# Two-layer attention trunk: weight loads woven between units, the row of 1/rms by a matmul with ones, five plain pairs, and earlier scores in layer 1

## The chip, the cores and the metric

One core of a Trainium2 chip runs the whole program in one launch. Its engines each have an instruction queue of their own: TensorE (PE, with PEld for its weight loads), VectorE (DVE), ScalarE (ACT), GpSimd (POOL) and SyncE (SP, which issues most transfers). They wait for one another through semaphores only. The metric is device time in microseconds; 0.2% of it is 2.8 us.

## The reference

The input is x, 512 tokens by 1024 channels. Two layers, each attention and then a dense FFN, both behind an RMSNorm and added to x; a final RMSNorm:

```
for i in range(2):
    h = rmsnorm(x, norm_mix[i])
    x = x + (window_gqa_sink(h, ...) if i == 0 else dilated_mixture_attention(h, ...))
    h = rmsnorm(x, norm_ffn[i])
    x = x + (silu(h @ w_gate[i]) * (h @ w_up[i])) @ w_down[i]      # 1024 -> 2816 -> 1024
return rmsnorm(x, norm_final)
```

Layer 0 is windowed attention with 16 query and 4 key heads. Layer 1 has three groups of heads (windows 128, 512 and 2048; strides 1, 4 and 16), each with its own q, k and v of 16 heads, merged by softmax weights.

## The kernel before, in words

All is held transposed, 128 channels by 512 tokens a tile. Each fp32 operand is split into a high and a low part (fp32r): ACT copies the high part, DVE subtracts to get the low one. `mm3` (L121) multiplies high by high, high by low and low by high, in pieces of 256 columns, so a `unit` (L204) of 128 output channels is 8 k-steps of 6 matmuls, 48 in all. `load` (L104) fetches a unit's weights (SP) and splits them: `wh` on ACT (L97), `wl` on DVE (L98). The weight pool has three buffers of each.

The order on PE is written out by hand everywhere: generators yield after each k-step (a slot), and `spread`, `weave` and `chain` put steps of attention between slots. The other engines are put in order by a scheduler that takes, among the instructions that are ready by its own clock, the one that comes first in the program. Only in the first part of each FFN are DVE and ACT kept in program order too (`ORDERED`, L855 and L931).

RMSNorm is put off: matmuls run on x times its gain, and results are scaled by 1/rms per token. `squares` (L263) adds up x*x in `ssum` (POOL). `norm_sums` (L296) sums over the channels by matmuls with one column of ones, which gives a number per token on partitions, and computes 1/rms there on tiles of 4 columns. `norm_rows` (L305) turns these into a row repeated on all partitions (`rb`) by four PE transposes and an ACT copy.

**Layer 0** runs k, q and v of the first heads, then attention in 16 blocks, each woven with a stretch of `fill` (L489): the other q and k units and the first output units. **Layer 1** runs q and k of group 0, then the four values units of group 0 (64 slots), then the attention steps `attention_a(0)` (scores, merge, turns, weighted sum) among further units (`fillers`, L1297). The numbers in `waits` (L1246) are the slots between the steps.

**The FFN** (`swiglu`, L585) has 22 pairs of a gate and an up unit. The first `plain` (6) pairs are plain units (`conventional`, L863). The others are made by a Strassen scheme of 7 products of half a unit's length, 12 matmuls each (`product`, L710), which needs sums and differences of the input, made on DVE in 19 steps (`input_steps`, L633: 8 `normed`, then splits `parts` and subtractions `less`) within the plain pairs, by `make`. Per pair f, in program order: load of up(f); `combined(f-1)` (two DVE multiplies); `make` or `kept(f-1)` (a split); load of gate(f+1); `gated(f)` (a DVE multiply and Silu); `make`. In the last plain pair, the weight sums of the first Strassen pair take the place of the loads: `h12 l12 f5`, `h64 l64 f7`, `h57 l57`, `h3 l3` (h on ACT, l and f on DVE). The third product of a Strassen pair uses `h57` and `l57`. Gate(1) and up(1) here mean the units of pair 1.

## Time and profile before

| | us |
|---|---|
| median of 3 runs | 1396.22 (1395.93 to 1396.76) |
| the profiled execution | 1396.07 |
| its span, first to last instruction | 1394.3 |
| PE busy in it | 1382.5 (99%) |
| DVE busy | 855.4 (61%) |
| ACT busy | 681.9 (49%) |
| POOL busy | 225.2 (16%) |

Busy PE is not PE at its peak: matmuls are pipelined, and one that is shown as 276 ns starts some 113 ns after the one before it. So read the starts of matmuls for its pace, and look at the gaps for its waits.

### The profile page before, as it was taken

The page shows a single profiled execution, that of the slowest core. Times are in us where ns is not written, and L with a number is a line of the kernel's source. Part 1 is how long each engine was busy: PE and PEld are TensorE (multiplying, and loading weights), DVE is VectorE, ACT ScalarE, POOL GpSimd, SP SyncE. Part 2 cuts the span into 40 slices and gives each one's busy share as a digit, 9 for nine tenths or more (in the row PEclk, how much of TensorE's full clock was granted, in tenths as well). Part 3 has the DMA queues.
Part 4 walks back from the last instruction along what each step waited for, and adds up shares of the span by engine and source line. Part 5 has one row for each costly group of instructions (what it writes and reads, how often), then busy time and mean ns, then how long its engine had stood idle before and what let it go on. Part 6 is the DMA issues. An engine that isn't in the chain of part 4 may idle for free.

```text
span 1394.3 us, 29677 instructions
## 1 busy us (share of the span) xinstructions
PE 1382.5 (99%) x12414; PEld 1367.2 (98%) x12414; DVE 855.4 (61%) x1593; ACT 681.9 (49%) x1250; POOL 225.2 (16%) x318
## 2 busy tenths in 40 slices
PE   9999999999999999999999999999999999999998
PEld 8988999999999999999999999999999999999998
DVE  6876558853687456345656556646466884388633
ACT  6866534632556356435545436436354462265522
POOL 1233320100110111011112111211132010021022
PEclk9999999999999999999999999999999999999999
DMA  6110263752683232322122222222136383387122
GB/s 203 61 62 16 77 184 104 188 138 99 183 201 92 89 110 94 107 77 92 62 93 80 73 92 76 78 83 71 62 110 179 112 212 105 106 210 194 65 95 73
DMA packets 61063, 153.63 MB, mean 110 GB/s; under 512 B 8320, under 2 KB 14336, under 8 KB 60928
## 3 DMA queue, kind: packets, MB, share of 16 engines
q1 hardware_dynamic: 49888, 134.28, 29.1%
q0 software_dynamic: 10752, 16.92, 7.6%
q8 instruction: 97, 1.59, 0.5%
q10 hardware_dynamic: 288, 0.52, 0.1%
q14 instruction: 38, 0.31, 0.1%
HBM read 149.52 MB, written 2.17 MB: 109 GB/s over the span
## 4 chain that ended last, share of the span: by engine, by line
PE 93%; DVE 3%; ACT 2%; issue 1%; SPq 0%; DMA 0%; POOL 0%; DVEq 0%; ACTq 0%
PE mm L126 38%; PE mm L714 12%; PE sc L126 11%; PE psv L126 9%; PE sc L714 9%; PE tp L126 5%; PE ov L431 1%; PE sc L1140 1%; PE ovb L1195 1%; PE sc L1081 1%; PE tp L1103 1%; ACT pr L407 1%; PE ov L1122 1%; DVE pr L400 1%; PE sc L148 1%; DVE wl L98 1%
## 5 line engine op out<-in xcount | busy, mean ns | idle before, releaser
L98 DVE TENSOR_TENSOR wl<-wraw,wh 128x1024 fp32r<-128x1024 f32 (+5 forms) x196 | 211.6, 1084 | 193.3 <-ACT wh L97 190.4
L97 ACT ACTIVATE wh<-wraw 128x1024 fp32r<-128x1024 f32 (+3 forms) x195 | 181.6, 937 | 240.4 <-PE mm L126 132.2
L126 PE MATMUL mm<-xh,wh 128*128 128x256 f32 x1320 | 267.2, 282 | 0.6 <-ACT xh L259 0.6
L126 PE MATMUL mm<-xl,wh 128*128 128x256 f32 x1320 | 260.9, 278 | 0.1
L126 PE MATMUL mm<-xh,wl 128*128 128x256 f32 x1320 | 260.5, 277 | 0.0
L126 PEld LDWEIGHTS mm<-xh,wh 128*128 128x128 f32 x1320 | 201.6, 189 | 2.5 <-ACT xh L259 0.9
L126 PEld LDWEIGHTS mm<-xl,wh 128*128 128x128 f32 x1320 | 201.0, 189 | 0.7 <-DVE xl L260 0.6
L126 PEld LDWEIGHTS mm<-xh,wl 128*128 128x128 f32 x1320 | 200.8, 189 | 0.0
L671 POOL DMA_DIRECT2D w<-wunits x64 | 56.1, 907 | 417.8 <-DVE wl L694 165.9
L126 PE MATMUL psv<-wh,xh 128*128 128x256 f32 x288 | 80.7, 280 | 0.0
L126 PE MATMUL psv<-wl,xh 128*128 128x256 f32 x288 | 79.9, 277 | 0.2 <-DVE wl L98 0.2
L126 PE MATMUL psv<-wh,xl 128*128 128x256 f32 x288 | 79.8, 277 | 0.0
L273 POOL TENSOR_TENSOR ssum<-ssum,tmp 128x512 f32<-128x512 f32 x26 | 45.8, 1762 | 180.3 <-ACT tmp L270 118.8
L714 PE MATMUL mm<-bh,wh 128*128 128x256 f32 x256 | 70.7, 276 | 0.0
L714 PE MATMUL mm<-bl,wh 128*128 128x256 f32 x256 | 70.7, 276 | 0.0
L714 PE MATMUL mm<-bh,wl 128*128 128x256 f32 x256 | 70.7, 276 | 0.0
L714 PE MATMUL sc<-bh,wh 128*128 128x256 f32 x256 | 70.7, 276 | 0.0
L714 PE MATMUL sc<-bl,wh 128*128 128x256 f32 x256 | 70.7, 276 | 0.0
L714 PE MATMUL sc<-bh,wl 128*128 128x256 f32 x256 | 70.7, 276 | 0.0
L714 PE MATMUL mm<-bh,h 128*128 128x256 f32 x256 | 70.7, 276 | 0.0
L714 PE MATMUL mm<-bl,h 128*128 128x256 f32 x256 | 70.7, 276 | 0.0
L714 PE MATMUL mm<-bh,l 128*128 128x256 f32 x256 | 70.7, 276 | 0.0
(242 smaller groups left out, 3716.0 us busy)
## 6 DMA issues: line engine op xcount, KB each, us to landing
wraw<-wunits SPq DMA_DIRECT2D x159, 512.0 KB, 3.2
w<-wunits SPq DMA_DIRECT2D x96, 256.0 KB, 4.9
w<-wunits POOLq DMA_DIRECT2D x64, 256.0 KB, 5.7
wraw<-wv SPq DMA_DIRECT2D x25, 512.0 KB, 3.3
wraw<-wunits SPq DMA_DIRECT2D x28, 192.0 KB, 2.4
x<-xT SPq DMA_DIRECT2D x8, 256.0 KB, 5.2
wraw<-wunits SPq DMA_DIRECT2D x3, 256.0 KB, 5.8
wraw<-wunits SPq DMA_DIRECT2D x2, 384.0 KB, 2.9
```

The lines of the kernel that those rows point to most:

```text
L97: nc.scalar.activation(out_h, src, AF.Copy)
L98: nc.vector.tensor_tensor(out_l, src, out_h.bitcast(F32), op=OP.subtract)
L126: nc.tensor.matmul(out[:, cols], a, b[:, cols], start=first and k == 0 and c == 0, stop=last and k == 2, skip_group_check=True)
L148: nc.tensor.matmul(outs[a], qp[a][:, qc], k[a][:, kc], start=first and k is kp, stop=k is low, skip_group_check=True)
L273: eng.tensor_tensor(norm["sum"], norm["sum"], sq, op=OP.add)
L400: nc.vector.tensor_tensor_reduce(out=pr[:, e, :w], in0=ps[hf], in1=tab0[:, off:off + w], scale=SLOPES[heads[e]], scalar=-3e38, op0=OP.add, ...
L407: nc.scalar.activation(pr[:, e, :w + 1], pr[:, e, :w + 1], AF.Exp, bias=m[:, 1, e:e + 1], accum_out=m[:, 2, e:e + 1])
L431: nc.tensor.matmul(ov[64 * hf:64 * hf + 64, 256 * n:256 * n + 256], v0[:, k0 // 128 + kb, vs], st["pt", kb][:, 256 * hf:256 * hf + 256], s ...
L671: nc.gpsimd.dma_start(sums[:, 512 * k:512 * k + 512], v[:, 0:512], accum_op=OP.add)
L714: nc.tensor.matmul(out, a[:, j], b[:, j], start=first and j == 0 and i == 0, stop=j == 3 and i == 2, skip_group_check=True)
L1081: nc.tensor.matmul(out, qk["qs", p][a][:, 128 * t:128 * t + 128], kp[k], start=t == ts[0] and k == 0, stop=k == 1, skip_group_check=True)
L1103: nc.tensor.transpose(tp[:, (nb * a + kb) * 128:(nb * a + kb) * 128 + 128], st["pr", p, ts][:, a, o + 128 * kb:o + 128 * kb + 128], ident)
```

## The change

1. In layer 0, the units behind the first values are built with `ahead=True` and chained by a new generator, `staggered`: it starts each next unit, and so its load, when the unit before is half done, and not when it ends. PE's order stays.
2. In both FFNs, `norm_direct` replaces `norm_sums` and `norm_rows`. It splits `ssum` into two parts (ACT, DVE), and four matmuls of 256 columns with a 128x128 tile of ones give the sum over channels on all partitions at once. 1/rms is then computed on 128x512 tiles (five DVE operations and one on ACT), where it was computed on 128x4 tiles. On PE it stands behind the first k-step of up(0). `gated(0)` and the first `normed` come before the rest of up(0).
3. `plain` is 5 instead of 6, in both FFNs.
4. In layer 1, the two scores and the merge of `attention_a(0)` come among the values units 2 to 4, and the slots between its later steps are reset. The number of slots up to its end stays at 49.

```
--- before.py
+++ after.py
@@ -189,6 +189,19 @@
                     gens.append(makers[k + 2]())
                     next(gens[-1][1])
                 yield
+
+    def staggered(n, gen, makers):
+
+
+        for make in (*makers, None):
+            for c in range(n):
+                if c == n // 2 and make:
+                    after = make()
+                    next(after[1])
+                next(gen)
+                yield
+            if make:
+                n, gen = after
 
     def last_outputs(out_part, at, fill=()):
 
@@ -311,6 +324,31 @@
         rb = norm["rb"] = spool.tile([128, S], F32, name="rb", bufs=1)
         cols = slice(128 * blocks[0], 128 * blocks[-1] + 128)
         nc.scalar.activation(rb[:, cols], pr[:, cols], AF.Copy)
+        for done in norm["wait"] or ():
+            done()
+        norm["wait"] = None
+
+    def norm_direct(pool, between):
+
+
+        ones_r = pool.tile([128, 512], F32R, name="l3")[:, 0:128]
+        nc.vector.tensor_scalar(ones_r, ident, 0.0, 1.0, op0=OP.mult, op1=OP.add)
+        parts = [pool.tile([128, 512], F32R, name="h3") for _ in range(2)]
+        split(*parts, norm["sum"])
+        between()
+        ps = bank("tp", "rrow")
+        for k, part in enumerate(parts):
+            for c in range(0, S, 256):
+                nc.tensor.matmul(ps[:, c:c + 256], ones_r, part[:, c:c + 256], start=k == 0 and c == 0, stop=k == 1,
+                                 skip_group_check=True)
+        rb = norm["rb"] = spool.tile([128, S], F32, name="rb", bufs=1)
+        v, t = [pool.tile([128, S], F32, name="us", bufs=4) for _ in range(2)]
+        nc.vector.tensor_scalar(v, ps, 1.0 / D, EPS, op0=OP.mult, op1=OP.add)
+        nc.scalar.activation(rb, v, AF.Sqrt)
+        nc.vector.reciprocal(rb, rb)
+        nc.vector.scalar_tensor_tensor(t, rb, -0.5, rb, op0=OP.mult, op1=OP.mult)
+        nc.vector.tensor_tensor(t, t, v, op=OP.mult)
+        nc.vector.scalar_tensor_tensor(rb, t, 1.5, rb, op0=OP.add, op1=OP.mult)
         for done in norm["wait"] or ():
             done()
         norm["wait"] = None
@@ -486,9 +524,10 @@
 
         early = values(0, 0, xh, xl, v0, "ov sc tp mm")[1]
         spread([norm_sums, 4, norm_rows], early)
-        fill = chain((16, early), q_unit(0, 2), q_unit(0, 3), k_unit(1),
-                     *[q_unit(1, i) for i in range(4)],
-                     *[out_part(j, 0, 4) for j in range(3)], *[out_part(j, 4, 6) for j in range(3)])
+        makers = [lambda i=i: q_unit(0, i, ahead=True) for i in (2, 3)] + [lambda: k_unit(1, ahead=True)]
+        makers += [lambda i=i: q_unit(1, i, ahead=True) for i in range(4)]
+        makers += [lambda j=j: out_part(j, 0, 4, ahead=True) for j in range(3)]
+        fill = chain((0, staggered(12, early, makers)), *[out_part(j, 4, 6) for j in range(3)])
 
         counts = [6, 7, 6, 5, 5, 5, 4, 4, 4, 4, 3, 2, 2, 2, 3, 2]
         units = [attention0(P, h, b) for P in range(2) for h in range(2) for b in range(4)]
@@ -853,12 +892,17 @@
                 return (raws.pop(f), *sums_of.pop(f))
 
             ORDERED = {mybir.EngineType.PE, mybir.EngineType.DVE, mybir.EngineType.Activation}
-            plain = 6
+            plain = 5
             parts = PARTS[n // 4]
             run(gate(0)[1])
-            norm_sums()
-            run(up(0)[1])
+            first_up = up(0)[1]
+            norm_direct(pool, lambda: next(first_up))
+            for _ in range(3):
+                next(first_up)
             steps = input_steps()
+            gated(0)
+            steps.pop(0)()
+            run(first_up)
 
             def conventional():
 
@@ -880,12 +924,9 @@
                         next(gen), next(gen)
                         if q == 0:
                             w = load_unit(wunits[u0 + 2 * f + 1], (NK, 128))
-                            if f == 1:
-                                norm_rows()
-                                gated(0)
                             combined(f - 1)
                             part["g"] = g
-                        elif q == 2 and f <= 3:
+                        elif q == 2 and f <= plain - 3:
                             kept(f - 1)
                         elif q:
                             make(1)
@@ -1243,7 +1284,7 @@
                      lambda: turn((0, 1), 0), lambda: turn((0, 1), 1), lambda: turn((2, 3), 2),
                      lambda: turn((2, 3), 3), weigh]
 
-            waits = {0: [6, 5, 5, 3, 12, 8, 8, 1], 7: [1, 4, 5, 4, 2, 3, 3, 9]}.get(p, [1, 4, 5, 4, 2, 4, 3, 9])
+            waits = {0: [0, 0, 0, 0, 16, 8, 8, 16], 7: [1, 4, 5, 4, 2, 3, 3, 9]}.get(p, [1, 4, 5, 4, 2, 4, 3, 9])
             return [w for pair in zip(waits, steps) for w in pair]
 
         def attention_b(p):
@@ -1291,8 +1332,12 @@
         run(gens[1])
         gens = [v_unit(pg, 0)[1] for pg in range(4)]
         spread([3, lambda: norm_rows(at=4)], gens[0])
-        for gen in gens:
-            run(gen)
+
+        run(gens[0])
+        firsts = attention_a(0)
+        others = chain(*[(16, gen) for gen in gens[1:]])
+        spread([4, *firsts[1:2], 10, *firsts[3:4], 16, *firsts[5:6]], others)
+        run(others)
 
         def fillers():
             line = []
@@ -1313,9 +1358,12 @@
 
 
         fill = fillers()
-        spread([1], fill)
         for p in range(8):
-            spread(attention_a(p), fill)
+            if p:
+                spread(attention_a(p), fill)
+            else:
+                spread(firsts[6:], fill)
+                spread([1], fill)
             first, second, rows = attention_b(p)
             if p < 7:
 
```

## Rows read from the trace of the kernel before

**Rows 1.** The page: the span, and busy time, share and instructions of each engine.

```profile
span 1394.3 us, 29677 instructions
...
PE 1382.5 (99%) x12414; PEld 1367.2 (98%) x12414; DVE 855.4 (61%) x1593; ACT 681.9 (49%) x1250; POOL 225.2 (16%) x318
```

**Rows 2.** Who PE waited for in the whole execution: total us, times, longest.

```profile
PE sc L148 <- DVE mst L400: 2.7, 2, 2.4
```

**Rows 3.** Stretches of layer 0's attention: length; busy us (instructions) of PE, PEld, DVE, ACT, POOL; granted PE clock; DMA share; GB/s.

```profile
98.00:101.00 3.00, 0.56 (x6) 0.36 (x4) 2.91 (x6) 1.32 (x3) 1.00 (x2) 0.99 0.39 113
101.00:104.40 3.40, 3.40 (x14) 3.30 (x14) 2.42 (x10) 1.31 (x4) 0.66 (x2) 0.51 0.13 54
```

**Rows 4.** The chain of work that ended last, in order of time, in the same place: start us, us, what.

```profile
96.63 0.96 ACT wh L97
97.61 1.21 DVE wl L98
...
99.58 0.69 DVE qt L136
100.92 1.65 PE sc L148 x4
```

**Rows 5.** Groups of instructions by line between 37 and 98.9 us, PE's and DVE's: count, busy us, mean ns, idle before.

```profile
L126 PE MATMUL mm<-xh,wh 128*128 128x256 f32 x102 | 21.9, 296 | 0.0
...
L98 DVE TENSOR_TENSOR wl<-wraw,wh 128x1024 fp32r<-128x1024 f32 x8 | 10.3, 1282 | 2.3 <-ACT wh L97 2.2
```

**Rows 6.** The same grouping for ACT over the whole execution: the splits of weights, and what ended ACT's idle time before them.

```profile
L97 ACT ACTIVATE wh<-wraw 128x1024 fp32r<-128x1024 f32 (+3 forms) x195 | 181.6, 937 | 240.4 <-PE mm L126 132.2 <-PE sc L126 59.0 <-issue 30.0
```

**Rows 7.** Timeline of PE at the start of the Strassen pairs of layer 0 (first products at 247.87, 249.22 and 251.94): start us, us, instruction.

```profile
247.87 0.28 PE L714 MATMUL mm<-bh,wh 128*128 128x256 f32 x1
...
249.22 0.28 PE L714 MATMUL sc<-bh,wh 128*128 128x256 f32 x1
...
251.94 0.28 PE L714 MATMUL mm<-bh,h 128*128 128x256 f32 x1
```

**Rows 8.** Stretches of PE around the norm of layer 0's FFN: the sums by ones, up(0), the transposes, the rest of gate(1), up(1). Length, busy us (instructions), granted clock, DMA share, GB/s.

```profile
187.77:188.58 0.81, 0.81 (x10) 1.00 0.92 369
188.58:194.32 5.74, 5.74 (x51) 1.00 1.03 262
...
195.73:196.09 0.36, 0.36 (x7) 1.00 1.04 285
196.09:200.26 4.17, 4.17 (x39) 1.00 1.11 244
200.26:205.71 5.45, 5.45 (x51) 1.00 0.64 162
```

**Rows 9.** Timeline of DVE in layer 0's FFN, from the norm to the first Strassen pair: start us, us, instruction, [idle before it, and what ended that].

```profile
188.84 1.23 DVE L98 TENSOR_TENSOR wl<-wraw,wh 128x1024 fp32r<-128x1024 f32 x1
...
197.07 0.69 DVE L618 TENSOR_TENSOR gs<-mm,rb 128x512 f32<-128x512 f32 x1 [5.95 <-ACT rb L313]
197.68 0.68 DVE L623 TENSOR_TENSOR us<-tp,rb 128x512 f32<-128x512 f32 x1
...
199.56 0.48 DVE L643 SCALAR_TENSOR_TENSOR h<-x,g_sb,rb 128x256 f32<-128x256 f32 x1
...
200.35 0.68 DVE L98 TENSOR_TENSOR al<-us,ah 128x512 fp32r<-128x512 f32 x1
...
219.58 1.22 DVE L98 TENSOR_TENSOR wl<-wraw,wh 128x1024 fp32r<-128x1024 f32 x1
220.72 0.69 DVE L623 TENSOR_TENSOR us<-tp,rb 128x512 f32<-128x512 f32 x1
...
222.05 1.22 DVE L650 SCALAR_TENSOR_TENSOR h<-h,l 128x1024 f32<-128x1024 f32 x1
...
229.62 1.23 DVE L98 TENSOR_TENSOR bl<-l,bh 128x1024 fp32r<-128x1024 f32 x1 [1.13 <-ACT bh L97]
...
246.64 1.22 DVE L694 TENSOR_TENSOR wl<-w,wh 128x1024 fp32r<-128x1024 f32 x1 [1.65 <-ACT wh L688]
...
249.60 1.83 DVE L694 TENSOR_TENSOR l<-w,h 128x1024 fp32r<-128x1024 f32 x2 [1.13 <-ACT h L688]
```

**Rows 10.** Timeline of ACT in the same place.

```profile
187.74 1.06 ACT L97 ACTIVATE wh<-wraw 128x1024 fp32r<-128x1024 f32 x1 [3.24 <-PE mm L126]
188.82 1.28 ACT L290 ACT_TABLE_LOAD   x1
...
199.67 0.63 ACT L97 ACTIVATE ah<-us 128x512 fp32r<-128x512 f32 x1 [0.76 <-DVE us L624]
```

**Rows 11.** Timeline of POOL: the last addition into ssum before layer 0's FFN.

```profile
184.65 1.79 POOL L273 TENSOR_TENSOR ssum<-ssum,tmp 128x512 f32<-128x512 f32 x1 [3.65 <-ACT tmp L270]
```

**Rows 12.** All reciprocals of L291: ns least, median, greatest; first and last start us; forms.

```profile
L291 DVE RECIPROCAL rstd<-rstd x6: 167/174/193, 26.6 to 1387.8; 128x4 f32<-128x4 f32 x3, 128x2 f32<-128x2 f32 x2, 128x8 f32<-128x8 f32 x1
```

**Rows 13.** Layer 1: the first scores' matmuls (ns least, median, greatest; first and last start us), the last split of group 0's first keys on ACT, and the stretch with the first scores, with columns as in the third group.

```profile
L1081 PE MATMUL sc<-ks,qs x64: 276/276/281, 582.9 to 971.4; 128*128 128x256 f32 x64
...
542.77 0.61 ACT L143 ACTIVATE kl<-kl 64x512 fp32r<-64x512 f32 x1
...
580.00:615.00 35.00, 35.00 (x303) 35.00 (x301) 13.15 (x35) 12.97 (x28) 3.61 (x6) 1.00 0.30 91
```

**Rows 14.** Timeline of DVE in layer 1's FFN, where it waits for rb.

```profile
1058.60 0.69 DVE L618 TENSOR_TENSOR gs<-mm,rb 128x512 f32<-128x512 f32 x1 [5.88 <-ACT rb L313]
```

## The prediction

> **What bounds the kernel now.** I read the page first: PE is busy 99% of the span [rows 1], so time is won only where PE has fewer matmuls, a better pace, or a wait that goes. Next the list of who PE waited for: one wait matters, 2.7 us on DVE in the scores of layer 0 [rows 2]. Then the stretches around it: PE does 0.56 us of work between 98 and 101, and in the 3.4 us behind it the granted clock is 0.51, the lower of its two levels (1.2 GHz, not 2.4), after PE had stood still [rows 3]. At half the clock 3.4 us of work would have taken 1.7, so the place costs 2.6 + 1.7 = 4.3 us. Everywhere else PE runs without a gap. A plain unit of 48 matmuls takes 5.45 us, 0.1135 each [rows 8], and a Strassen product of 12 takes 1.35 [rows 7].
>
> **Part 1, staggered loads.** The wait in layer 0 hangs on a weight split: ACT's `wh` at 96.63, DVE's `wl` at 97.61, only then the split of q and DVE's reading of the scores that PE waits for [rows 4]. A load that came half a unit earlier would take this away if the split stood where the program has it. It doesn't. Between 37 and 98.9 us PE did 102 / 16 = 6.4 units, and DVE split the weights of 8 [rows 5]; the first unit's weights were there before, so weights for nine are ready while the seventh is in work. Over the whole run, ACT's idle time before such a copy was ended mostly by PE [rows 6], by a unit that ended and freed one of three buffers. The copies thus start when a buffer comes free, two units ahead of need, and moving their place in the program by half a unit moves neither. SP's transfers run ahead in the same way. PE's order is unchanged. I take 0; the ends are -4.3 (the wait and the slow clock go) and +4.3 (another like it appears), since the order of ACT and DVE there is the scheduler's.
>
> **Part 2, the norm on PE.** From the first sum by ones (187.77) to up(1) (200.26) PE takes 12.49 us for two units and the norm [rows 8]. Two units are 10.90, so the norm costs 1.59: 0.81 for the sums, 0.36 for the transposes, and 0.42 because the matmuls between them run slower (up(0): 5.74 for 48). The change puts four matmuls of 256 columns there: 4 x 0.1135 = 0.45. It gains 1.14, or 0.72 if the slower pace stays; it was there between the sums and the transposes only, both of which go, so I take 1.14. PE could now wait for the split of `ssum`. POOL ends at 186.44 [rows 11]; a copy of 0.63 on ACT [rows 10] and a subtraction of 0.69 on DVE [rows 9] make 187.8. PE asks after gate(0) and one k-step, at 187.77 + 0.68 = 188.45. The cover is 0.6 us: nothing to pay, unless ACT takes the next `wh` (187.74 to 188.8 [rows 10]) first. Then PE waits 1.6.
>
> **Part 3, one plain pair less.** 96 matmuls become 84 in each FFN: 12 x 0.1135 = 1.36 us off PE. But the plain pairs cover the 19 steps that DVE owes to the Strassen input, and now four pairs must do it, not five. What it owes has to be counted.
>
> When DVE starts: it waits for `rb` until 197.07 now, idle for 5.95 us [rows 9]. The new chain fills this gap. With the result of the ones at 189.1 and the split of up(1)'s weights first (188.84 [rows 9]): v to 190.67, root (0.63) to 191.3 behind the table load, which ends at 190.1 [rows 10], reciprocal, three operations of 0.72 with their handover, `gated(0)` 0.61, first `normed` 0.79 (199.56 to 200.35 [rows 9]). The reciprocal is not in the trace at 512 columns. It takes 167 ns for 2, 174 for 4 (median) and 193 for 8 [rows 12], 4.3 ns a column, so 2.4 us; the ends are 0.69, a plain operation of that shape [rows 9], and 4.4, twice the slope. By this `combined(0)` begins at 197.3, or at 196.9 if v comes before the split; it began at 197.68 [rows 9].
>
> How much it owes from there to the end of `l57`: 20 operations on 1024 columns at 1.14 (6 `wl`, 7 `parts`, 4 `less`, `l12`, `l64`, `l57`), 7 `normed` at 0.79, 4 `combined` at 1.33, 8 of 512 columns at 0.61 (spacings of [rows 9]): 22.8 + 5.5 + 5.3 + 4.9 = 38.5 us. The same count for before is 22, 8, 5 and 10, 44.2 us, and the trace has 53.1 from 197.68 to the end of `l57` at 250.74, so 8.9 of waits. Of these, four stand behind ACT whatever PE does: 1.13 twice, where a split follows its own subtraction, 1.65 before `l64` and 1.13 before `l57` (one of each kind in [rows 9]), 5.0 together. The rest waited for PE or other copies and shrinks when DVE is behind: 0 to 3.9, I take 1.3. So DVE ends `l57` 44.8 us after its start, between 241.7 and 242.1.
>
> When PE wants it: gate(1) starts at 187.77 + 5.45 + 0.45 = 193.67, eight units end at 237.27, two products go before the last quarter of up(4), and the third product begins at 240.0 and wants the low part 0.2 later. **`l57` comes 1.5 to 1.9 us late**; I take 1.8. In before it had 1.4 to spare (product at 251.94 [rows 7]). With the waits at their ends it is 0.2 to 4.5. Part of it will show one unit earlier, as up(4) waiting for its `wl`.
>
> The sum for an FFN is -1.36 - 1.14 + 1.8 = -0.7. Layer 1's FFN has the same order, and DVE waits there for `rb` as long (5.88 [rows 14]), so twice: -1.4.
>
> **Part 4, layer 1.** The same 49 slots and the same matmuls, in another order; PE has no gap in the stretch they leave [rows 13], so there is nothing to win. The keys are split by 543.4, and the first scores, now at 582.9 [rows 13], move forward by 3 + 48 slots of 0.68 us to 548: 4.8 us of cover. ACT and DVE are busy 13 of 35 us where the steps come from; the values leave about the same. The merge's transfers move ahead on POOL's queue, which is busy 3.6 of 35 us and has nobody behind it. I take 0; a badly placed step costs what the one in layer 0 does, up to 4.3.
>
> **The time.** 1396.07 - 1.4 = 1394.7 for the profiled execution, whose span of 1394.3 leaves 1.8 around it; the median of the runs lies 0.15 higher: **1394.8**.
>
> **The rivals.** *DVE is in time*: the chain is shorter (reciprocal near 0.69) or the waits shrink more, and `l57` is late by 0 to 0.6. Then -1.9 to -2.5 for an FFN, 1391.2 to 1392.4. For it: DVE's idle time of 5.95 is there to be used. Against: the count above. *Staggering moves the splits*, and the wait in layer 0 goes: 4.3 more, 1390.5. For it: the wait hangs on just such a split. Against: [rows 5, 6]. *The reciprocal is slow*, the rival on the other side: if a column takes eight times the 1.04 ns that it takes in a plain operation ((1.22 - 0.69) us / 512 columns [rows 9]), 512 take 4.3 us, `l57` is 3.7 late, and each FFN loses 1.2: 1398.6, and up to 1401.8 where PE also waits 1.6 for the split of `ssum`. It decides from a reciprocal of 3.1 us on. For it: the slope rises with the size, 3.5 ns a column from 2 to 4 and 4.8 from 4 to 8 [rows 12]; against: it would have to double. *The scheduler's new order makes a new wait* in layer 0 or 1 with a slow clock behind it: +4.3, 1399.1.
>
> The Trainium skill bears on the slow reciprocal ("VectorE: DVE Perf Modes", section "First, the fixed hardware budget"): it says that the reciprocal divides iteratively, with a repeat count of 8. If that means eight passes for each column, 512 columns take 4.3 us and the change is slower by that rival; the slope of [rows 12] is half of it, so the trace bears it out no further than as a rival.
>
> **How the numbers follow.** Forecast 0.47, with its own range 1393.0 to 1396.8 (`l57` late by 0.9 to 2.8); DVE in time 0.20; staggering works 0.12; slow reciprocal 0.13; new wait 0.08. A measurement of this kernel tells about 0.2% from no change, 2.8 us: faster is below 1393.4, slower above 1399.0. Faster: 0.20 + 0.12 + 0.05 from the forecast's lower edge = 0.37. Slower: 0.08 of the reciprocal's cases and 0.06 of the new wait's = 0.14. Same: 0.49. The range leaves out the tails of the second, third and fourth case: 1390.3 to 1399.6.
>
> **What would show it.** Right: PE waits for DVE's `wl` or `l57` at the first Strassen pair of each FFN, about 1.8 us in each, and up(0) at 5.45 a unit; layer 0 as before up to 150 us, slow clock included; a reciprocal of 2.4 us. Wrong: no such wait (then 1391 to 1392), layer 0 without its gap, a reciprocal over 3 us, or PE waiting for the split of `ssum`.

## The result and the profile after

The changed kernel takes 1399.82 us, median of 20 executions (1396.94 to 1412.29), beside 1396.54 for the kernel before (20 executions on the same chip, 1394.09 to 1398.35). The ratio is 1.0041, 95% interval 1.0026 to 1.0056: slower by 0.4%. The forecast was 1394.8 with a range up to 1399.6, so the median lies just outside, and on the other side of no change. The executions fall into two groups: 15 at 1396.9 to 1401.9 (median 1399.45) and 5 at 1410.2 to 1412.3. The profiled one took 1398.51, in the lower group.

The page: the span is 2.4 us longer than in [rows 1], although PE has 40 instructions fewer and is busy 1.0 us less.

```profile
span 1396.7 us, 29646 instructions
...
PE 1381.5 (99%) x12374; PEld 1365.0 (98%) x12374; DVE 872.1 (62%) x1607; ACT 687.2 (49%) x1260; POOL 227.0 (16%) x322
```

Who PE waited for (total us, times, longest). The wait of [rows 2] is still there, and a new one stands above it.

```profile
PE mm L753 <- ACT gs L765: 3.1, 2, 1.5
PE sc L148 <- DVE mst L438: 2.7, 2, 2.4
```

Timeline of PE where it belongs, the first Strassen pair of layer 0 (L753 is the product, L714 before). The third product, which began without a gap in [rows 7], starts 1.70 us late at 243.27, and a later one into the same bank 0.40 late at 250.58.

```profile
241.35 0.39 PE L126 MATMUL tp<-xh,wl 128*128 128x256 f32 x2
243.27 0.38 PE L753 MATMUL mm<-bh,h 128*128 128x256 f32 x1 [1.54 <-ACT gs L765]
...
250.58 0.39 PE L753 MATMUL mm<-bh,h 128*128 128x256 f32 x1 [0.24 <-ACT us L765]
```

The list names ACT's `gs`, the copy that empties the bank `mm`, which the first product filled and the third adds to. ACT's timeline bears it out: that copy ends at 243.22, and PE goes 0.05 later, as soon as it does where one engine alone keeps it waiting (e15 below, at 233.65). On ACT the copy stands behind `h57` and `h3` (first row) and one more, and `h57` had waited 1.90 us for DVE's `f7`.

```profile
240.85 1.58 ACT L727 ACTIVATE h<-w 128x1024 fp32r<-128x1024 f32 x2 [1.90 <-DVE w L739]
...
242.86 0.36 ACT L765 ACTIVATE gs<-mm 128x256 f32<-128x256 f32 x1
```

DVE's timeline has the chain ahead of that. `f7` ends at 240.82, and `l57`, the first of the two operations in the last row, at 243.17, only 0.05 before ACT's copy (243.09 as the prediction counts, by the start of the next operation). So both ways to the third product begin at `f7`: one by `h57` and `l57`, the other by `h57` and ACT's queue. No run parts the two. The rows also show the new norm. The 5.95 us that DVE waited in [rows 9] are filled, its chain runs from the split of `ssum` to `l57`, and only ACT makes it wait.

```profile
189.79 0.68 DVE L346 TENSOR_SCALAR us<-rrow 128x512 f32<-128x512 f32 x1
191.17 3.35 DVE L348 RECIPROCAL rb<-rb 128x512 f32<-128x512 f32 x1 [0.70 <-ACT rb L347]
194.56 0.69 DVE L349 SCALAR_TENSOR_TENSOR us<-rb 128x512 f32<-128x512 f32 x1
...
196.74 0.69 DVE L657 TENSOR_TENSOR gs<-mm,rb 128x512 f32<-128x512 f32 x1
...
198.14 0.68 DVE L662 TENSOR_TENSOR us<-tp,rb 128x512 f32<-128x512 f32 x1
...
238.99 1.22 DVE L733 TENSOR_TENSOR wl<-w,wh 128x1024 fp32r<-128x1024 f32 x1 [1.65 <-ACT wh L727]
240.13 0.69 DVE L739 TENSOR_TENSOR w<-w,wraw 128x512 f32<-128x512 f32 x1
241.95 1.82 DVE L733 TENSOR_TENSOR l<-w,h 128x1024 fp32r<-128x1024 f32 x2 [1.13 <-ACT h L727]
```

Stretches of PE (columns as in [rows 3]): gate(1) behind the ones, then the wait. Gate(1) takes 5.66 at a granted clock of 1.00, where a unit took 5.45 in [rows 8].

```profile
193.67:199.33 5.66, 5.66 (x51) 5.66 (x49) 5.42 (x9) 0.63 (x1) 1.73 (x2) 1.00 1.11 264
241.46:243.27 1.81, 0.28 (x3) 0.08 (x1) 1.32 (x2) 1.81 (x5) 0.00 (x0) 1.00 0.92 226
```

So PE has two paces at one clock. From start to start a 256-column matmul takes 113.4 ns (its row shows a mean of 276) or 117.8 (281). In the changed kernel the slower one reaches from the ones to 234.3, 46 us, in layer 0, and as far in layer 1. In the kernel before it ended with the transposes.

Where the time went: FFN means here from the end of gate(0) to the start of the last matmul of its Strassen products. It takes 275.54 us before (187.77 to 463.31), 277.21 and 277.18 after: +1.67 and +1.64. Layer 1's attention is 1.00 shorter. Together +2.3, the span's +2.4.

### The profile page after: what moved, and what is told of

It reads as the page before. It is cut to its first block, busy times and chain, and to the rows that moved or that the text cites. A ratio compares the mean times of both kernels' runs of the same rounds, so it can differ in the third digit from the quotient of the medians.

```text
span 1396.7 us, 29646 instructions
## 1 busy us (share of the span) xinstructions
PE 1381.5 (99%) x12374; PEld 1365.0 (98%) x12374; DVE 872.1 (62%) x1607; ACT 687.2 (49%) x1260; POOL 227.0 (16%) x322
## 4 chain that ended last, share of the span: by engine, by line
PE 86%; DVE 8%; ACT 4%; issue 2%; DMA 0%; POOL 0%; DVEq 0%; SPq 0%; ACTq 0%
PE mm L126 34%; PE mm L753 13%; PE sc L753 10%; PE psv L126 9%; PE sc L126 8%; PE tp L126 2%; DVE wl L98 2%; PE ov L469 1%; PE sc L1181 1%; PE ovb L1236 1%; PE sc L1122 1%; PE tp L1144 1%; ACT pr L445 1%; DVE bl L98 1%; PE ov L1163 1%
## 5 line engine op out<-in xcount | busy, mean ns | idle before, releaser
L98 DVE TENSOR_TENSOR wl<-wraw,wh 128x1024 fp32r<-128x1024 f32 (+4 forms) x192 | 207.7, 1086 | 183.2 <-ACT wh L97 179.9
L97 ACT ACTIVATE wh<-wraw 128x1024 fp32r<-128x1024 f32 (+5 forms) x191 | 177.3, 935 | 239.5 <-PE mm L126 128.6
L126 PE MATMUL mm<-xh,wh 128*128 128x256 f32 x1288 | 261.4, 283 | 0.5 <-ACT xh L272 0.5
L126 PE MATMUL mm<-xl,wh 128*128 128x256 f32 x1288 | 255.0, 278 | 0.0
L126 PE MATMUL mm<-xh,wl 128*128 128x256 f32 x1288 | 254.6, 278 | 0.0
L126 PEld LDWEIGHTS mm<-xh,wh 128*128 128x128 f32 x1288 | 196.8, 189 | 2.4 <-ACT xh L272 0.8
L126 PEld LDWEIGHTS mm<-xl,wh 128*128 128x128 f32 x1288 | 196.5, 189 | 0.3 <-DVE xl L273 0.3
L126 PEld LDWEIGHTS mm<-xh,wl 128*128 128x128 f32 x1288 | 196.4, 189 | 0.0
L753 PE MATMUL mm<-bh,h 128*128 128x256 f32 x272 | 75.5, 278 | 3.3 <-ACT gs L765 3.1
L753 PE MATMUL mm<-bh,wh 128*128 128x256 f32 x272 | 75.1, 276 | 0.0
L753 PE MATMUL mm<-bl,wh 128*128 128x256 f32 x272 | 75.1, 276 | 0.0
L753 PE MATMUL mm<-bh,wl 128*128 128x256 f32 x272 | 75.1, 276 | 0.0
L753 PE MATMUL sc<-bh,wh 128*128 128x256 f32 x272 | 75.1, 276 | 0.0
L753 PE MATMUL sc<-bl,wh 128*128 128x256 f32 x272 | 75.1, 276 | 0.0
L753 PE MATMUL sc<-bh,wl 128*128 128x256 f32 x272 | 75.1, 276 | 0.0
L753 PE MATMUL mm<-bl,h 128*128 128x256 f32 x272 | 75.1, 276 | 0.0
L753 PE MATMUL mm<-bh,l 128*128 128x256 f32 x272 | 75.1, 276 | 0.0
L286 POOL TENSOR_TENSOR ssum<-ssum,tmp 128x512 f32<-128x512 f32 x26 | 44.8, 1722 | 181.1 <-ACT tmp L283 181.0
```

The lines of the kernel that those rows point to most:

```text
L97: nc.scalar.activation(out_h, src, AF.Copy)
L98: nc.vector.tensor_tensor(out_l, src, out_h.bitcast(F32), op=OP.subtract)
L126: nc.tensor.matmul(out[:, cols], a, b[:, cols], start=first and k == 0 and c == 0, stop=last and k == 2, skip_group_check=True)
L286: eng.tensor_tensor(norm["sum"], norm["sum"], sq, op=OP.add)
L753: nc.tensor.matmul(out, a[:, j], b[:, j], start=first and j == 0 and i == 0, stop=j == 3 and i == 2, skip_group_check=True)
```

## The experiments

Two theories. **T1**: DVE's chain, up to `f7` and then by `l57` or by ACT's copy, sets the start of the third product; it is longer than forecast, and what PE does meanwhile is hidden. **A**: the loss is PE's slower pace, which the ones start and nothing ends. A rival to both (B) has five pairs as the cause of the pace. FFN lengths, in us, measured alike in every trace:

| kernel | FFN layer 0 | layer 1 | median, ratio [95%] |
|---|---|---|---|
| before | 275.54 | 275.54 | 1396.54 |
| changed | 277.21 | 277.18 | 1399.82, 1.0041 [1.0026, 1.0056] |
| e1 norm by ones alone | 276.23 | 276.24 | 1397.55, 1.0044 [1.0021, 1.0068] |
| e2 five pairs alone | 281.59 | 281.57 | 1413.83, 1.0124 [1.0092, 1.0157] |
| e3 changed, transposes in `tp` | 277.24 | 277.22 | 1399.84, 1.0027 [1.0018, 1.0037] |
| e4 layer 1's scores alone | 275.54 | 275.54 | 1395.09, 0.9989 [0.9980, 0.9997] |
| e5 before, sums added | 284.88 | 284.89 | 1419.82, 1.0170 [1.0157, 1.0183] |
| e6 e5 and transposes | 277.07 | 277.22 | 1400.61, 1.0030 [1.0018, 1.0042] |
| e7 changed, no Newton | 283.70 | 283.70 | 1415.64, 1.0116 [1.0076, 1.0156] |
| e10 early transposes, five | 275.13 | 275.13 | 1394.73, 1.0007 [0.9987, 1.0027] |
| e11 early transposes, six | 275.28 | 275.38 | 1394.74, 0.9985 [0.9976, 0.9994] |
| e12 staggered alone | 275.54 | 275.54 | 1396.14, 1.0002 [0.9994, 1.0011] |
| e13 e10, new order | 274.02 | 274.02 | 1392.37, 0.9975 [0.9966, 0.9984] |
| e14 changed, turns, order | 283.38 | 275.00 | 1415.36, 1.0130 [1.0106, 1.0154] |
| e15 changed, turns | 277.23 | 277.23 | 1400.18, 1.0052 [1.0030, 1.0074] |

(Medians and intervals mix both groups where a kernel has two; the lengths are those of the profiled execution.)

**The parts alone.** The norm by ones, with six pairs:

```diff
-            norm_sums()
-            run(up(0)[1])
+            first_up = up(0)[1]
+            norm_direct(pool, lambda: next(first_up))
...
-                            if f == 1:
-                                norm_rows()
-                                gated(0)
...
```

> The kernel before with the row of 1/rms by ones alone (six plain pairs, old attention order). Theory A (the matmuls of the ones put PE into its slow pace of 117.8 ns a matmul, and no transposes come to end it): the matmuls behind the row run at 117 to 118 ns until PE next waits; six plain pairs are about 57 us, so 57 x 0.04 = 2.2 us lost against 1.1 gained by the shorter norm, +1.0 per FFN and +2 in all; more if nothing ends the pace before the Strassen products. DVE has a pair more to work behind, so no wait at the third Strassen product. Rival B (the slow pace comes of five pairs or of DVE's load, not of the row): the pace is 113.5 behind the row and the kernel gains 1.1 to 1.6 per FFN, -2.3 to -3. Rival C (all of the loss was DVE being late): the same gain, -2.3.

Seven executions at 1396.5 to 1397.8, five at 1407.9 to 1410.2. PE doesn't wait at the third product, yet each FFN is 0.7 longer where it should be 1.1 shorter: the matmuls have a mean of 281 between 200 and 230, and keep this pace to 234.8. With six pairs and DVE in time the pace costs about what A says, +1.4 in the two FFNs, not +2, and B falls.

Five pairs with the old norm:

```diff
-            plain = 6
+            plain = 5
...
-                        elif q == 2 and f <= 3:
+                        elif q == 2 and f <= plain - 3:
```

> The kernel before with five plain pairs instead of six and nothing else. Theory A: the transposes stay, so the pace is 113.5 behind them; PE waits at the third Strassen product for DVE's l57, by the 1.8 us of the changed kernel, less the 1.1 that the longer norm lets PE ask later, plus the 0.4 to 1.0 by which rb comes later: 1.1 to 1.8 us. With 1.36 off PE that is -0.3 to +0.4 per FFN, and between -0.6 and +0.8 in all. Rival B (five pairs cause the slow pace): matmuls at 117.8 over the plain part, +1.7 more per FFN, +3 in all. Rival C (DVE's lateness is the whole loss): +1.6 per FFN, +3.3 in all.

Far slower than any theory had it: 6 us in each FFN. PE's waits, and the stretch behind the third product:

```profile
PE mm L714 <- ACT gs L726: 5.1, 2, 2.7
...
PE tp L126 <- ACT wh L97: 2.6, 2, 1.4
PE tp L126 <- DVE wl L98: 1.4, 2, 0.7
```

```profile
246.79:250.33 3.54, 3.54 (x20) 3.54 (x18) 3.50 (x6) 1.35 (x3) 1.15 (x2) 0.52 0.90 187
```

DVE is later still (PE waits 2.84 us at the third product, 2.2 in up(4)), though not for `rb`: it uses that 9.30 us after the end of gate(0), in the changed kernel 9.16. But from there to `l57` it takes 49.5 us instead of 46.4, since it stands behind ACT for 9.0 instead of 5.9. What differs is the order of the steps: the change puts `gated(0)` and the first `normed` earlier, and e10 below, which does so with the old norm, stands behind ACT for 5.9 too. No run tries these places alone. Behind the longer wait the granted clock is 0.52, the level of 1.2 GHz, for 3.5 us. Behind the changed kernel's 1.70 it stayed at 1.00. Three of the six executions took 12 us more.

The staggered loads, and layer 1's scores:

```diff
...
-        fill = chain((16, early), q_unit(0, 2), ...
+        makers = [lambda i=i: q_unit(0, i, ahead=True) for i in (2, 3)] + ...
+        fill = chain((0, staggered(12, early, makers)), ...
```

> The kernel before with the staggered loads of layer 0 alone. The prediction's step: 0, the wait of 2.6 us before the scores at 98 us and the slow clock behind it stay; 1395.5 to 1397. Rival: the staggering has a gain that other parts of the change hid, up to -4.3.

0, as forecast: the wait in layer 0 and the slow clock behind it stay (PE stands still for 2.42 us of the first stretch, 2.44 in [rows 3]), and ACT's copy of the weights starts at 96.82, against 96.53 in the kernel before, as much later as the whole stage.

```profile
98.50:101.20 2.70, 0.28 (x3) 0.07 (x1) 2.60 (x6) 1.14 (x2) 0.80 (x2) 1.00 0.39 112
101.20:104.60 3.40, 3.39 (x16) 2.88 (x16) 2.39 (x10) 1.31 (x4) 0.57 (x2) 0.61 0.16 65
```

```diff
-        for gen in gens:
-            run(gen)
+        run(gens[0])
+        firsts = attention_a(0)
+        others = chain(*[(16, gen) for gen in gens[1:]])
+        spread([4, *firsts[1:2], 10, *firsts[3:4], 16, *firsts[5:6]], others)
+        run(others)
...
```

> The kernel before with layer 1's first scores moved among the values, and nothing else. By the shift between the traces layer 1's attention gains 1.0 us, since PE's slow pace of 577.8 to 609.5 (31 us at 4% is 1.2) does not come: -1.0 us in all. Rival: the gain belongs to other parts of the change (the state in which PE leaves the FFN of layer 0), and the move alone does nothing: 0, as the prediction had it.

-1.0, not 0. Between 579 and 609 the kernel before runs at the slower pace; with the scores elsewhere it doesn't, though the matmuls are the same. First before, then e4:

```profile
L126 PE MATMUL mm<-xl,wh 128*128 128x256 f32 x62 | 12.4, 281 | 0.0
```

```profile
L126 PE MATMUL mm<-xl,wh 128*128 128x256 f32 x64 | 12.5, 276 | 0.0
```

**Is the pace what the change lost?** Transposes behind the ones should end it. The first try:

```diff
+        turned = bank("tp", "turned")
+        for b in range(4):
+            nc.tensor.transpose(turned[:, 128 * b:128 * b + 128], ident, ident)
```

> The changed kernel with four transposes of the identity into a spare bank right behind the matmuls of the ones; their result is not used. Theory A (transposes end the slow pace, as those of the row did in the kernel before): up(0) to up(4) run at 113.5 ns, the plain part takes 1.7 us less in each FFN, the transposes cost 0.4, and PE then asks earlier, so that part of the gain turns into a longer wait for DVE (up to 1.3): between -0.1 and -1.3 per FFN against the changed kernel, its time about 1397.5 to 1399.5. Rival (what ended the pace in the kernel before was a wait of PE, not the transposes): 117.8 still, +0.4 per FFN, 1400.6.

The plain part runs at 113.4 then, and nothing is won. The bank made PE wait 1.64 first, so this run could not tell. The same with a bank that is free (`bank("ov", "turned")`):

> The changed kernel with four transposes of the identity behind the matmuls of the ones, this time into a bank that nobody uses there, so that PE doesn't wait for it. T1 (DVE's chain sets the third Strassen product, the slow pace is hidden in the wait): plain part at 113.5 ns, PE comes 1.3 earlier less 0.5 for the transposes, and the wait at the third product grows from 1.7 to 2.5 or more; no gain for the executions near 1399, and up to 2 us lost per FFN if the clock falls behind the longer wait: 1398 to 1402. Theory A (the slow pace is what was lost): -1 per FFN, 1396.5 to 1397.5. Both: no executions at 1410, unless the wait itself leaves the slow pace behind.

This one tells. PE's plain part is fast, PE comes earlier, and waits for it all. The waits, then a `wl` of DVE and PE's timeline, with the wait that this `wl` ended:

```profile
PE mm L756 <- ACT gs L768: 3.1, 2, 1.5
...
PE tp L126 <- DVE wl L98: 1.3, 2, 0.6
...
PE mm L126 <- DVE wl L98: 0.4, 2, 0.2
```

```profile
232.37 1.22 DVE L98 TENSOR_TENSOR wl<-wraw,wh 128x1024 fp32r<-128x1024 f32 x1
```

```profile
233.65 0.50 PE L126 MATMUL tp<-xh,wl 128*128 128x256 f32 x2 [0.63 <-DVE wl L98]
...
241.26 0.39 PE L126 MATMUL tp<-xh,wl 128*128 128x256 f32 x2
243.19 0.39 PE L756 MATMUL mm<-bh,h 128*128 128x256 f32 x1 [1.54 <-ACT gs L768]
```

The third product starts at 243.19, against 243.27, the FFN takes 277.23, against 277.21, and seven executions lie at 1398.2 to 1401.0, five at 1407.1 to 1413.5. A falls for the lower group: DVE's chain sets the start. (T1's longer wait is spread: 0.36 and 0.80 in units before, 1.70 here, 0.38 behind.)

**Is it DVE's chain?** The three Newton operations left out, so that the correction of 1/rms is missing in the FFNs:

```diff
...
         nc.vector.reciprocal(rb, rb)
-        nc.vector.scalar_tensor_tensor(t, rb, -0.5, rb, op0=OP.mult, op1=OP.mult)
-        nc.vector.tensor_tensor(t, t, v, op=OP.mult)
-        nc.vector.scalar_tensor_tensor(rb, t, 1.5, rb, op0=OP.add, op1=OP.mult)
```

> The changed kernel without the three Newton operations on 512 columns behind the reciprocal (the correction of 1/rms is left out of the FFNs), which makes DVE's chain 2.2 us shorter in each. Theory T1 (the third Strassen product starts when DVE has l57, since DVE works without a gap for PE from the reciprocal on, and the reciprocal's 3.35 us makes it that late): l57 comes 2.2 us earlier, PE's wait of 1.7 at the third product goes, and the small waits around it; -1.7 to -2.1 per FFN, 1395 to 1396.5 for most executions. Rival A alone (the slow pace of PE is what the change lost): PE arrives no sooner, the wait is for something else, 0. Either way the slow pace starts at the ones and may outlast the plain part more often, since fewer waits end it: then +10 in an FFN.

The wait at the third product is gone:

```profile
241.66 0.40 PE L126 MATMUL tp<-xh,wl 128*128 128x256 f32 x2
241.90 0.28 PE L750 MATMUL mm<-bh,h 128*128 128x256 f32 x1
```

But five of six executions take 1414.7 to 1416.7. Only one, which was not profiled, shows the gain that T1 forecast: 1395.8. In the profiled one (1416.3) the slower pace, which the ones started, reaches through the whole FFN in both layers; no wait interrupts PE any more. Groups of lines between 260 and 460:

```profile
L750 PE MATMUL sc<-bh,wh 128*128 128x256 f32 x112 | 31.5, 281 | 0.0
```

**What does the pace cost alone?** Four one-column sums in the kernel before, behind the plain part (result not used):

```diff
                         first, lead = conventional()
+                        ps = bank("ov", "extra")
+                        for b in range(4):
+                            nc.tensor.matmul(ps[:, b:b + 1], ident, ones, start=b == 0, stop=True, ...)
```

> The kernel before with four sums (one fp32 column each, of the identity, into a spare bank, not used) behind the plain part of each FFN, about 248 us in layer 0; in the kernel before nothing interrupts PE from there to the end of the FFN, some 260 us on. Theory A (such sums put PE into the pace of 117.8 ns, and it keeps that until something interrupts it): 4% of 260 us in each FFN, +10 us, and +21 in all with 0.6 for the sums themselves. This would also be the +11 us that some executions of the changed kernel and of the two edits show. Rival D (the pace ends by itself, or the Strassen products don't have it): +0.6 to +1 per FFN, under +2 in all.

> The same sums and behind them four transposes of the identity into the spare bank, not used. Theory A: the transposes put PE back into the pace of 113.4; 0.6 for the sums and 0.5 for the transposes per FFN, +2.2 in all. Rival (transposes don't end the pace; in the kernel before it ended because PE had waited): +21 or more.

+23.7 for the sums, +4.5 when transposes follow them. From 250 to 460 us, the kernel before, then e5: 70 matmuls fewer in the same 210 us at the same clock, 8.2 us.

```profile
250.00:460.00 210.00, 210.00 (x1855) 210.00 (x1854) 142.66 (x199) 103.70 (x161) 22.70 (x26) 1.00 0.56 152
```

```profile
250.00:460.00 210.00, 210.00 (x1785) 210.00 (x1784) 138.69 (x192) 101.46 (x154) 22.68 (x26) 1.00 0.55 147
```

In e6, 1.5 and 1.7 of the 4.5 lie in the FFNs. Another 1.4 are layer 1's attention, where the slower pace begins at 1008.8 and in this execution reached the FFN; in the kernel before it ended at 1013.8.

**What the executions at 1410 have.** The changed kernel itself, profiled three times more:

> The changed kernel as it is, one more profiled execution. If it falls near 1410: the matmuls of one FFN have a mean of 281 ns from the first Strassen pairs to its end, those of the other 276, and the waits for DVE are as in the first profile. If that group had another cause: 276 in both and a new wait or a lower granted clock of 11 us. Near 1399 it says nothing of that group.

> As the run before it: another profiled execution of the changed kernel, to catch one near 1410; the same two readings.

> As the two runs before it: another profiled execution of the changed kernel, to catch one near 1410; the same two readings.

1399.4, 1422.0 and 1400.9: none lies near 1410 itself. The second has both FFNs at 285.6, 8.4 longer, with the waits at the third products as before. Stretches of layers 0 and 1, the first profile and then this one:

```profile
250.00:460.00 210.00, 209.76 (x1851) 209.57 (x1850) 141.85 (x198) 102.79 (x160) 22.61 (x26) 1.00 0.56 153
1130.00:1340.00 210.00, 210.00 (x1855) 210.00 (x1855) 133.41 (x186) 96.93 (x149) 20.28 (x23) 1.00 0.51 138
```

```profile
250.00:460.00 210.00, 210.00 (x1783) 209.81 (x1783) 138.55 (x193) 102.08 (x154) 22.60 (x26) 1.00 0.57 151
1130.00:1340.00 210.00, 210.00 (x1786) 210.00 (x1785) 136.09 (x190) 99.20 (x150) 22.19 (x26) 1.00 0.55 144
```

In layer 0 of that execution the pace turned slow at the third product's wait and stayed. What one slow FFN costs is read from e14's profile below: 8.4 us in layer 0's FFN and 2.7 in the attention behind it, 11.1 together, and the two groups of the changed kernel lie 10.9 apart. That the executions at 1410 have one slow FFN is inferred from this, not seen. The first of the three settles A in the changed kernel itself: there the ones left PE at the faster pace in layer 0 (mean 277 from 200 to 230, against 281), PE waited 0.74 and 0.79 in the units before, 1.70 at the third product, and the FFN took 277.21 all the same.

```profile
242.23 0.39 PE L126 MATMUL tp<-xh,wl 128*128 128x256 f32 x2
244.16 0.39 PE L753 MATMUL mm<-bh,h 128*128 128x256 f32 x1 [1.54 <-ACT gs L765]
```

**A cure.** The norm of the kernel before with its transposes in the middle of up(0), five pairs, layer 1's scores:

```diff
-            run(up(0)[1])
+            first_up = up(0)[1]
+            for _ in range(4):
+                next(first_up)
+            norm_rows()
...
```

> Five plain pairs and layer 1's early scores with the norm of the kernel before (sums, four columns, transposes), its transposes moved from gate(1) to the middle of up(0), behind four of its eight steps. The 1/rms of four columns was ready at 191.1 there and PE came for it at 195.7; now rb comes at about 192.6, 4 us before it does in the changed kernel. T1: l57 comes 4 us earlier than in the changed kernel, at 239, before PE asks at 240.5, so no wait at the third product; -1.36 for the pair and -0.2 for the shorter slow stretch per FFN, -0.9 in layer 1, together -4: 1392.0. The transposes end the slow pace, so no executions 10 us longer. Rival A' (five plain pairs are too few whatever the norm): DVE waits for PE's products instead, l57 late by 1 to 2, -1 in all. A wait of PE for the four columns would cost 0 to 0.5 per FFN.

DVE uses `rb` first 5.1 us after the end of gate(0), in the changed kernel 9.2, and the row's cost on PE falls. PE still waits 0.48 at the third product and 0.13 behind it, and between the two runs slowly. Nine executions at 1393.0 to 1396.4, three at 1405 to 1406. -0.4 per FFN, not -1.6: once `rb` is early, DVE waits for PE's products (0.56, 0.63, 0.45 in its timeline), as A' said. Then the steps of the last pair's weights, so that DVE no longer stands behind ACT for 1.65 and 1.13:

```diff
-                            for m in (("h12", "l12", "f5"), ("h64", "l64", "f7"), ("h57", "l57"), ("h3", "l3"))[q]:
+                            for m in (("h12", "l12", "h64", "f5", "f7"), ("h57", "l64"), ("l57",), ("h3", "l3"))[q]:
```

> The early transposes of the norm before with five plain pairs and layer 1's early scores, and the same new order of the weight steps. T1: the waits of 0.48 and 0.13 at the third product and behind it go, and with them the 7.6 us at the slow pace between them and the executions 10 us longer: -1.0 per FFN against that kernel, 1392 to 1393 in all executions. Rival: h64's copy waits for a buffer of the unit in work, ACT's next steps stand behind it, and the wait only moves: 1394.5.

DVE's timeline, then PE's: `l57` ends at 239.2, and the third product follows without a gap.

```profile
236.30 1.21 DVE L694 TENSOR_TENSOR wl<-w,wh 128x1024 fp32r<-128x1024 f32 x1
238.04 1.83 DVE L694 TENSOR_TENSOR l<-w,h 128x1024 fp32r<-128x1024 f32 x2 [0.52 <-ACT h L688]
```

```profile
240.89 0.39 PE L126 MATMUL tp<-xh,wl 128*128 128x256 f32 x2
...
241.12 0.28 PE L714 MATMUL mm<-bh,h 128*128 128x256 f32 x1
```

1392.37, all ten executions between 1391.2 and 1394.1: faster than both kernels, by 0.25% than the one before. Six pairs with the early transposes:

> Early transposes and layer 1's early scores with six plain pairs, so that DVE has a pair more to work behind. If the pair is worth its 12 matmuls once DVE is in time, this kernel is slower than the one with five pairs and the new order of the weight steps by 2 x 1.36 = 2.7, less or more by nothing else: 1395.0, and no executions 10 us longer. If that kernel's gain comes of the order alone, this one is at 1392.5 to 1393.5.

1394.74. The FFNs are 1.26 and 1.36 longer than with five, so the pair is worth its 1.36 where DVE is in time. (The medians, each beside its own runs of the kernel before, are 1.8 apart, less than the 2.7 expected.)

The same order and the transposes put into the changed kernel:

> The changed kernel with the transposes into the free bank and with the last plain pair's weight steps in another order: both sums (f5, f7) and the second copy (h64) come ahead of the two subtractions (l64, l57), so that DVE does not stand behind ACT for 1.65 and 1.13 us. T1: l57 ends 2.8 us earlier, at 240.3 on the changed kernel's scale, and PE, at the fast pace, asks at 240.5: no wait at the third product, -2.8 - 0.4 per FFN, 1392 to 1393.5, with no executions 10 us longer. If only the pace matters, 1396.5 to 1397.5; if the third product waits for something else than DVE's chain, 1398 to 1400.

The wait at the third product goes here too, but 1405.8 to 1418.8: PE still waits for the `wl` of the units before, and in layer 0 of the profiled execution PE left a hitch of 0.1 us at the slower pace and kept it to the end of the FFN (a mean of 281 from 260 to 460; 276 in layer 1, whose FFN took 275.00).

```profile
248.98 0.28 PE L756 MATMUL sc<-bh,wl 128*128 128x256 f32 x1
249.10 0.38 PE L756 MATMUL mm<-bh,h 128*128 128x256 f32 x1
249.31 0.28 PE L756 MATMUL mm<-bl,h 128*128 128x256 f32 x1
```

## Why the prediction was wrong

- **Part 1, staggered: 0.** Right, and for its reason; e12 has it alone, with the copies where they were. (The wait and its clock cost 2.4 + 1.7 = 4.1 by [rows 3], not 4.3.)
- **Part 3, `l57` late: the failed step.** The mechanism and its place were right, the size was not. Forecast 1.8, in an FFN of -0.7. Measured against a PE without slow pace (460 matmuls at 0.1134 from 187.58, so 239.7), the third product starts 3.5 late, and 0.6 comes behind it, 0.4 of that at 250.58, a wait that the forecast had not: +2.3, which turns -0.7 into the 1.67 measured, but for rounding. The largest piece is the **reciprocal**: taken at 2.4 us by the slope of [rows 12], measured 3.35. With it `combined(0)` began at 198.14, not at 196.9 to 197.3; from there to `l57` DVE took 44.95 us, where 44.8 was forecast, so the count of its operations and waits was right. The forecast gave 3.1 as the point from which the slow rival decides, so that rival came true, at less than its 4.3. (Its 1398.6 beside the profiled 1398.51 is in part luck: each FFN lost 0.5 more than its 1.2, and layer 1's attention gave 1.0 back.) A second piece was in no term: the first matmul of the product waits for ACT's copy out of its bank. By `l57` alone, which is wanted 0.2 into the product, it could have started at 243.0, so this is 0.3. The rest are pieces of 0.1 to 0.2: gate(0) ended 0.2 earlier, and `l57` takes 0.1 longer to reach PE than counted. That DVE's chain sets the product is shown by e15 and e7 from two sides; that the reciprocal's excess is about half of the 1.7 that was missed at the third product is read from its row, not tried by itself.
- **Part 2, the slow pace: "both of which go, so I take 1.14".** Wrong: in 5 of the 8 profiled FFNs of the changed kernel the plain part ran slowly behind the ones, to 46 us, past the lower bound of 0.72. In the lower group this cost nothing, since the wait for DVE's chain hid it (277.2 with it and without it). With six pairs it did cost (e1, 0.7 longer instead of 1.1 shorter).
- **The upper group** was in no case of the forecast. A wait or the ones can leave PE at the slower pace, and where nothing interrupted it in the profiles (e7, e14, the execution at 1422) it stayed to the end of the FFN, 8.4 us in each of the last two. The kernel before has its transposes last and no wait of PE behind them, and e5 and e6 show that sums put there cost it as much, unless transposes follow.
- **Part 4, layer 1: 0.** Wrong, -1.0: the stretch of [rows 13] has no gap, but it has the slower pace (281 for its matmuls, e4 276). A busy PE was taken for a PE at its best.
- The sum: 2 x 1.67 - 1.0 = 2.3 in the profile, where -1.4 was forecast. The lower group's median is 2.9 above the kernel before, and the upper group raises it by another 0.4.

The Trainium skill ("VectorE: DVE Perf Modes", section "First, the fixed hardware budget") gives the reciprocal's divide a repeat count of 8. Read as eight passes for each column, that was an estimate of 4.3 us. The row has 3.35, between this and the slope's 2.4: (3.35 - 0.19) us / 504 columns beyond the 8 of [rows 12] is 6.3 ns, six times the 1.04 of a plain operation.

## What to carry to other kernels

Before work goes off a full engine, add up what its feeder owes until the first handover, with each operation's price at the size that it will have: by the slope from 2 to 8 columns the reciprocal cost 2.4 us at 512, and it took 3.35. A gain on PE counts only if the feeder is in time, and when it is late, first look where it stands behind another engine: a new order of five small steps was worth 1.1 us per FFN here (e13 beside e10). The same goes for the copy that empties a bank: it was late here because it stood behind other work on ACT. Look at the time from matmul to matmul too: an engine that is 99% busy can run 4% slower for hundreds of microseconds.

## What was not expected of the hardware

- Matmuls of one form run at 113.4 or 117.8 ns from start to start, at a granted clock of 1.00. The pace holds until something interrupts PE: through 210 us and more in e5, e7 and the execution at 1422.
- Four one-column fp32 sums were followed by the slower pace in 17 of the 18 profiled FFNs that begin with them, and behind those added in e5. In the other one, e11's layer 0, PE came into them at the slower pace and left at the faster one. Behind the transposes of 1/rms in these FFNs, and behind those of the identity in e6, the pace was the faster one. Transposes elsewhere don't always: those that end at 1007 are followed by the slower pace, before and after. The four matmuls of the ones turned the pace over in all 8 profiled FFNs of the changed kernel, from the faster to the slower in 5 and back in 3. A wait leaves either; the same wait of 1.70 was followed by the faster one in layer 0 of the first profile and by the slower one in layer 1. What decides is open.
- After waits of 1.70 the granted clock stayed at 1.00; after 2.84 us of waiting, in e2, with 2.2 of shorter waits in the unit before, it was 0.52 for 3.5 us.
